# Where the prompt's softmax transposes stand in a neighbourhood-attention loop

## The chip, the cores and the metric

The kernel runs on one core of one Trainium2 chip. The metric is the device time of one execution in microseconds; the number given for a kernel is the median of its runs. Engines are called by the short names of the profile: PE (TensorE, matrix products and transposes), PEld (its weight loads), ACT (ScalarE), DVE (VectorE), POOL (GpSimd), SP (SyncE, here a queue of transfers).

## The reference, cut to what matters

Two layers work on 128 prompt tokens and 1024 sample tokens of width 1024. Layer 0 projects the tokens, runs a depthwise convolution branch (A) and an attention branch (B), gates both and projects back. Layer 1 is a pooling mixer. The change lies in branch B of layer 0, which has two parts with 8 heads of 64:

```python
# prompt: plain attention over the 128 prompt tokens
s = einsum('bqhd,bkhd->bhqk', q, k) * ATT_SCALE
o = einsum('bhqk,bkhd->bqhd', softmax(s), v)
# sample: a clamped 8 x 16 window on a grid of width 64, plus all context keys, in one softmax
s = concatenate([s_win + bias (masked), s_ctx]); p = softmax(s)
o = einsum(p_win, v_win) + einsum(p_ctx, v_ctx)
```

The sample's attention is far larger than the prompt's: 64 score tiles of 128 x 512 against 8 of 128 x 128.

## The kernel before, in words

The work before the attention (input projections, convolution, normalisation) and behind it (output projection of layer 0, layer 1) is nearly all matrix products on PE. The attention itself is a loop written out by hand, `attention_steps` (L1002). Heads are taken in 4 pairs (`pr`), each pair in 4 steps, so there are 16 steps `s` = 0 to 15 and a closing pass 16; `i` = `s % 4`.

A step `s` works on three things at once, in this order on PE:

- the scores of step `s + 1` (L879, 12 products of 128 x 512 into four "mm" banks; DVE adds the bias and takes the row minimum at L884; ACT takes the exponentials at L891; DVE and POOL normalise at L895 and L897);
- the values of step `s - 1` (L912, 32 products into one "cv" bank, which DVE multiplies into the gate at L923, the function `gate`);
- the transposes of the probabilities of step `s` (`turn`, L903): two tiles into the "tp" banks, which ACT copies out (L1055), one tile into a "cv" bank (ACT, L1061), and one more into a "tp" bank (DVE, L1062).

There are two "cv" and two "tp" banks, each handed out in turn, so a tile waits until the reader of the tile two before it in that tag is done.

Into each step two small pieces are woven. For pairs 0 to 2 these are five pieces that prepare the next pair (`prep`: transposes of its queries and keys) and three pieces of the prompt's attention (`prompt_attention`): `first` makes the two score tiles of the prompt (L937, one "cv" and one "tp" bank), DVE takes maxima (L939, L940), ACT the exponentials (L942), and then DVE and POOL normalise them (L945, L947) in a tile `pp`; `second` transposes `pp` on PE (L954) into one bank, and DVE copies it back (L955); `third` multiplies by the values (L960) and DVE gates the result (L965). A step has two places for a piece: place a, between the scores of the next step and the values ("cv" bank), and place b, ahead of the last transpose group ("tp" bank). In pairs 0 to 2 `first` stands in place b of the third step, `second` in place a of the fourth, `third` in place b of the fourth. In the last pair, which has no next pair to prepare, the three stand in place a of its first, second and third step (s = 12, 13, 14).

The order on PE, ACT and DVE inside the attention is the order in which the code issues (`manual_schedule`, L998). The order on POOL and on SP's transfer queue is made by a planner that goes by modelled times. From s = 10 on, the loop also converts the right half of the output weights (`load_right`, L1080 and on): POOL writes the high part (L1101), DVE the low part (L1102), from two buffers that SP refills (L1090) once both have read them. From s = 14 on, DVE and ACT also split the first output tiles (L1117, L1118), and in s = 15 and 16 PE does products of the output projection ahead (L1132).

Of the kernel before, what the change touches and what calls it, by code (L numbers as in the profile page):

```python
# [46 lines left out]
def _body(tc, nc, A, O, const, wp, arena, tmpp, smp, psp):  # L47
# [10 lines left out]
    def bank(tag):  # L58
        return psp.tile([P, 512], F32, tag=tag, bufs={"mm": 4, "tp": 2, "cv": 2}[tag], name=nm(tag))
# [123 lines left out]
    def split(raw, n=WUNIT, c=256):  # L183
        hi = wp.tile([P, WUNIT], F32R, tag="whi", bufs=4, name=nm("whi"))
        lo = wp.tile([P, WUNIT], F32R, tag="wlo", bufs=4, name=nm("wlo"))
        se.copy(hi[:, :n], raw[:, :n])  # L186
        ve.tensor_tensor(lo[:, :n], raw[:, :n], f(hi[:, :n]), ALU.subtract)  # L187
        return hi.rearrange("p (k c) -> p k c", c=c), lo.rearrange("p (k c) -> p k c", c=c)
# [563 lines left out]
    def bias_load(pr, hf):  # L752
        runs = ((0, 5), (5, 6), (6, 7), (7, 8)) if hf == 0 else ((0, 1), (1, 2), (2, 3), (3, 4), (4, 8))
        for e in range(2):
            h = 2 * pr + e
            for a, b in runs:
                off = 128 + RS[0][a] * 32 if hf == 0 else (RS[1][a] - 4) * 32
                m = 7 - DR0[hf][a]
                sy.dma_start(
                    bias[hf, e][a * 16 : b * 16, :, off : off + 256],  # L760
                    EX[m : m + b - a, :, :, h, :].rearrange("m q j k -> (m q) j k"),
                )
# [101 lines left out]
    def scores(step):  # L864


        pr, hf, j0 = step
        qh, ql, kh, kl, _ = qkT[pr]
        o = 0 if hf == 0 else 512
        ps, sts = [], []  # L870

        def matmuls(i):
            j = j0 + i
            bs = [bank("mm"), bank("mm")]
            qo = slice(hf * 512 + j * P, hf * 512 + (j + 1) * P)
            for n, (q, k) in enumerate(((qh, kh), (qh, kl), (ql, kh))):
                for e in range(2):
                    kv = k[H[e], o : o + 1024].rearrange("p (r c) -> p r c", c=64)[:, :, CB[j] : CB[j] + 32]
                    te.matmul(bs[e].rearrange("p (r c) -> p r c", c=32), q[H[e], qo], kv, start=(n == 0), stop=(n == 2))  # L879
            ps.append(wp.tile([P, 2, 512], F32, tag="whi", bufs=4, name=nm("p")))  # L880
            sts.append(small(8, "st"))
            for e in range(2):

                ve.tensor_tensor_reduce(  # L884
                    out=ps[i][:, e, :], in0=bs[e], in1=bias[hf, e][:, JT[j], :], scale=-1.0, scalar=3e38, op0=ALU.add, op1=ALU.min,
                    accum_out=sts[i][:, e : e + 1],
                )

        def exp(i, e):
            p, st = ps[i][:, e, :], sts[i]  # L890
            se.activation(p, p, AF.Exp, bias=st[:, e : e + 1], scale=-1.0, accum_out=st[:, 2 + e : 3 + e])  # L891

        def norm(i):
            st = sts[i]
            ve.reciprocal(st[:, 4:6], st[:, 2:4])  # L895
            for e in range(2):
                gp.tensor_scalar(ps[i][:, e, :], ps[i][:, e, :], st[:, 4 + e : 5 + e], 0.0, ALU.mult, ALU.add)  # L897

        return matmuls, exp, norm, ps

    def turn(tb, p):
        for x in range(4):
            te.transpose(out=tb[:, x * P : (x + 1) * P], in_=p[:, x * P : (x + 1) * P], identity=ident)  # L903
# [89 lines left out]
    def new_pt():  # L993
        return [wp.tile([P, 2, 512], F32, tag="wlo", bufs=4, name=nm("pt")) for _ in range(2)]
# [6 lines left out]
    def attention_steps():  # L1001

        nonlocal gr
        n = len(STEPS)
        sc_, vw, pts = {0: hold["S"]}, {0: hold["V"]}, {}
        right = load_right(0, (13, 15, 17, 2, 3, 4))
        for s in range(n + 1):
            i, pr = s % 4, s // 4  # L1010
            last_ = pr == 3
            nxt = None
            if s + 1 < n:
                nxt = sc_[s + 1] = scores(STEPS[s + 1])
                nxt[0](0)
                nxt[0](1)
                if pr < 3 and i in (0, 2):
                    bias_load(pr + 1, i // 2)
            if i == 0 and pr < 4:
                pieces = prep(pr + 1) if pr < 3 else []  # L1020
                prompt = prompt_attention(pr)
                ab = ([*prompt, None], [None] * 4) if last_ else ((pieces[0], pieces[2], pieces[4], prompt[1]), (pieces[1], pieces[3], prompt[0], prompt[2]))
            if s == n - 2:
                zs_part(0, 0)
            if s == n - 1:
                zs_part(0, 1)
                zs_part(1, 0)
                zs_part(1, 1)
            if s == n:
                out0_ahead(1)  # L1030
                units[L0_AT] = [split(*r) for r in raws[L0_AT]]
            if nxt:
                nxt[1](0, 0)
            a = ab[0][i]("cv") if s < n and ab[0][i] else None
            gate = values(STEPS[s - 1], pts.pop(s - 1), vw[STEPS[s - 1][0]]) if s else None
            if nxt:
                nxt[1](0, 1)
                nxt[1](1, 0)
            if a:
                a()  # L1040
            if nxt:
                nxt[2](0)
            if gate:
                gate()
            if s == n - 1:
                out0_ahead(0)
            if s == n:
                break
            ps = sc_.pop(s)[3]
            pt = pts[s] = new_pt()  # L1050
            tbs = [bank("tp"), bank("tp"), bank("cv")]
            for x in range(3):
                turn(tbs[x], ps[x // 2][:, x % 2, :])
            for x in range(2):
                se.copy(pt[0][:, x, :], tbs[x])  # L1055
            if nxt:
                nxt[1](1, 1)
            b = ab[1][i]("tp") if ab[1][i] else None
            tb = bank("tp")
            turn(tb, ps[1][:, 1, :])  # L1060
            se.copy(pt[1][:, 0, :], tbs[2])  # L1061
            ve.tensor_copy(pt[1][:, 1, :], tb)  # L1062
            if nxt:
                nxt[2](1)
            if b:
                b()
            if i == 2 and pr < 3:
                vw[pr + 1] = v_load(pr + 1)
            if n - 6 <= s < n - 1:
                hold["R"] = next(right)  # L1070
            if s == n - 3:
                gr = gr_tile()
                hold["gate"] = load_gates(0)
                y_of(0)
                y_of(1)
            if s == n - 2:
                raws[L0_AT] = load_raw(items[L0_AT][0])


    def load_right(l, ids, ahead=2):  # L1080


        hi = [slot(i, F32R, "wrh").rearrange("p (k c) -> p k c", c=512) for i in ids[:3]]
        lo = [slot(i, F32R, "wrl").rearrange("p (k c) -> p k c", c=512) for i in ids[3:]]
        rvs = []

        def load(k0):
            raw = wp.tile([P, WUNIT], F32, tag="raw", bufs=2, name=nm("raw"))
            rvs.append(raw.rearrange("p (k c) -> p k c", c=512))
            sy.dma_start(rvs[-1], A[f"w_out_{l}"][k0 * P : (k0 + 2) * P, 512:1024].rearrange("(k p) c -> p k c", p=P))  # L1090

        for k0 in range(0, 2 * ahead, 2):
            load(k0)
        yield hi, lo
        for k0 in range(0, 8, 2):
            rv = rvs[k0 // 2]
            for k in (k0, k0 + 1):
                if k % 2 and l:
                    se.copy(hi[k // 3][:, k % 3, :], rv[:, k - k0, :])
                else:  # L1100
                    gp.tensor_scalar(hi[k // 3][:, k % 3, :], rv[:, k - k0, :], 1.0, 0.0, ALU.mult, ALU.add)  # L1101
                ve.tensor_tensor(lo[k // 3][:, k % 3, :], rv[:, k - k0, :], f(hi[k // 3][:, k % 3, :]), ALU.subtract)  # L1102
            if k0 + 2 * ahead < 8:
                load(k0 + 2 * ahead)
            yield hi, lo
# [44 lines left out]
    def zs_part(t, kh):  # L1150
        g, a = t // 3, (t % 3) * P
        if t not in zs0:
            zs0[t] = [slot(i, F32R, "zs")[:, :D].rearrange("p (k t) -> p k t", t=P) for i in ((5, 8), (7, 9))[t % 2]]
        zpart(zs0[t], (zc, za)[kh][g][:, :, a : a + P], kh)

    def out0_ahead(t):

        first_out[t] = out_right(zs0[t], hold["R"])
# [200 lines left out]
    for i in range(len(items)):  # L1359
        a, b = ahead.get(i, (1, 2))  # L1360
# [35 lines left out]
```

## Time and profile before

| what | us |
|---|---|
| median of 3 runs (988.17 to 989.96) | 989.32 |
| profiled execution | 989.12 |
| its span, first to last instruction | 987.4 |
| PE busy | 949.5 (96%) |
| DVE busy | 603.0 (61%) |
| ACT busy | 404.9 (41%) |
| POOL busy | 368.4 (37%) |

PE is busy nearly throughout, so the time hangs on two things: how many microseconds PE works and where it stands still. The attention loop lies between about 443 and 563 us of the span. In the views, a line of the timeline gives the start, the length, the engine, the line of the code, the operation with its operands, the count of instructions merged into the row, and in brackets how long the engine was idle before it and what ended the wait. Matrix products are pipelined, so a merged row's length overlaps the next row's start a little; differences of starts are the safer measure.

### The profile page before, as it was taken

How to read it: one execution, taken by the hardware profiler on the slowest of the kernel's cores; microseconds unless marked ns; L12 is line 12 of the kernel's file. 1: busy time of each engine (PE TensorE's matmuls, PEld its weight loads, DVE VectorE, ACT ScalarE, POOL GpSimd, SP SyncE). 2: the span in 40 equal slices, each digit the busy share in tenths (PEclk: the TensorE clock that was granted, in tenths of full speed). 3: DMA queues.
4: the chain of work that ended last, by engine and by line, in shares of the span. 5: the costliest groups of instructions: out<-in, count | busy, mean ns of one | idle time of the engine just before them, and what ended most of it. 6: DMA issues, size and time to landing. Idle time of an engine off the chain costs nothing.

```text
span 987.4 us, 16652 instructions
## 1 busy us (share of the span) xinstructions
PE 949.5 (96%) x6388; PEld 863.0 (87%) x6388; DVE 603.0 (61%) x1243; ACT 404.9 (41%) x815; POOL 368.4 (37%) x485
## 2 busy tenths in 40 slices
PE   4887999999999999998998999999999999999998
PEld 2686988899999999986776788889999999998887
DVE  3577999999763444456776557566434545585332
ACT  3374666765411244238775423335222222231010
POOL 2264888998843301024455255341000000003322
PEclk8998999999999999999999999999999999999999
DMA  9969654226111111134334422151101111133311
GB/s 299 332 209 291 232 178 144 85 87 235 46 46 46 47 43 43 35 89 134 108 106 142 144 91 107 56 190 43 33 22 43 54 44 54 64 107 106 129 64 65
DMA packets 87531, 108.54 MB, mean 110 GB/s; under 512 B 10700, under 2 KB 73036, under 8 KB 87339
## 3 DMA queue, kind: packets, MB, share of 16 engines
q1 hardware_dynamic: 82539, 95.93, 30.6%
q0 software_dynamic: 2576, 9.18, 2.4%
q10 hardware_dynamic: 2336, 2.36, 0.7%
q8 instruction: 50, 0.82, 0.3%
q14 instruction: 30, 0.25, 0.1%
HBM read 94.64 MB, written 21.57 MB: 118 GB/s over the span
## 4 chain that ended last, share of the span: by engine, by line
PE 88%; DMA 7%; SPq 2%; DVE 1%; ACT 1%; issue 1%; POOL 1%; DVEq 0%; ACTq 0%; POOLq 0%
PE mm L232 37%; PE mm L239 16%; PE mm L1132 10%; PE mm L1125 10%; PE cv L912 3%; PE tp L903 2%; DMA wada<-in_w_ada 2%; PE mm L879 2%; PE mm L1295 2%; DMA tbias<-in_rpb 2%; PE tp L342 2%; DMA vwin<-in_cache_v 1%; DMA wad<-in_w_ada 1%; DMA raw<-in_w_out 1%; DMA raw<-in_w_in 1%; PE cv L903 1%
## 5 line engine op out<-in xcount | busy, mean ns | idle before, releaser
L232 PE MATMUL mm<-h,whi 128*128 128x384 f32 x1536 | 397.2, 338 | 1.7 <-ACT whi L186 1.4
L232 PEld LDWEIGHTS mm<-h,whi 128*128 128x128 f32 x1536 | 276.3, 188 | 9.0 <-ACT gr L474 2.6
L232 PE MATMUL mm<-h,wlo 128*128 128x384 f32 x768 | 257.3, 336 | 0.3 <-DVE wlo L187 0.3
L476 POOL TENSOR_TENSOR zc<-zc,gr 128x384 f32<-128x384 f32 x138 | 150.5, 1092 | 31.1 <-ACT gr L474 17.9
L239 PE MATMUL mm<-whi,h 128*128 128x256 f32 x864 | 157.1, 284 | 0.0
L232 PEld LDWEIGHTS mm<-h,wlo 128*128 128x128 f32 x768 | 144.3, 188 | 1.3 <-issue 0.7
L239 PEld LDWEIGHTS mm<-whi,h 128*128 128x128 f32 x864 | 135.1, 192 | 3.9 <-ACT gr L474 2.6
L239 PE MATMUL mm<-wlo,h 128*128 128x256 f32 x432 | 122.2, 283 | 0.0
L187 DVE TENSOR_TENSOR wlo<-raw,whi 128x1024 fp32r<-128x1024 f32 (+1 forms) x56 | 69.2, 1237 | 54.8 <-ACT whi L186 53.7
L487 DVE SCALAR_TENSOR_TENSOR cv<-u,convw,cv 128x384 f32<-128x384 f32 (+2 forms) x208 | 95.1, 513 | 0.9
L1132 PE MATMUL mm<-wrh,zs 128*128 128x512 f32 x288 | 92.4, 392 | 0.3 <-POOL wrh L1101 0.3
L1125 PE MATMUL mm<-whi,zs 128*128 128x512 f32 (+1 forms) x304 | 92.5, 379 | 0.0
L186 ACT CAST whi<-raw 128x1024 fp32r<-128x1024 f32 (+1 forms) x56 | 56.8, 1017 | 66.9 <-PE mm L232 23.6
L239 PEld LDWEIGHTS mm<-wlo,h 128*128 128x128 f32 x432 | 82.9, 192 | 0.0
L1139 POOL TENSOR_TENSOR y<-y,og 128x512 f32<-128x512 f32 x34 | 48.6, 1430 | 83.6 <-DVE og L1137 80.5
L474 ACT ACTIVATE gr<-u,convw 128x384 f32<-128x384 f32 (+2 forms) x128 | 64.3, 531 | 30.8 <-POOL zc L476 30.3
L897 POOL TENSOR_SCALAR p<-p,st 128x512 f32<-128x512 f32 x64 | 48.5, 771 | 49.6 <-DVE st L895 33.7
L1125 PEld LDWEIGHTS mm<-whi,zs 128*128 128x128 f32 x304 | 56.0, 188 | 10.7 <-issue 0.2
L1132 PEld LDWEIGHTS mm<-wrh,zs 128*128 128x128 f32 x288 | 53.9, 188 | 12.0 <-POOL wrh L1101 0.8
L1137 DVE TENSOR_TENSOR og<-mm,gr 128x512 f32<-128x512 f32 x34 | 23.3, 688 | 58.9 <-PE mm L1132 34.8
L1125 PE MATMUL mm<-wlo,zs 128*128 128x512 f32 (+1 forms) x152 | 57.2, 378 | 0.0
L456 ACT ACTIVATE th<-mm 128x384 f32<-128x384 f32 x48 | 23.5, 489 | 81.6 <-PE mm L232 81.5
(214 smaller groups left out, 1376.3 us busy)
## 6 DMA issues: line engine op xcount, KB each, us to landing
raw<-in_w_in SPq DMA_DIRECT2D x28, 512.0 KB
wad<-in_w_ada SPq DMA_DIRECT2D x16, 768.0 KB
wada<-in_w_ada SPq DMA_DIRECT2D x16, 512.0 KB
raw<-in_w_in SPq DMA_DIRECT2D x32, 256.0 KB
raw<-in_w_out SPq DMA_DIRECT2D x16, 512.0 KB
y0scr<-y POOLq DMA_DIRECT2D x9, 512.0 KB, 3.1
y<-y0scr SPq DMA_DIRECT2D x9, 512.0 KB
x<-in_x_sample SPq DMA_DIRECT2D x8, 512.0 KB
```

The lines of the kernel that those rows point to most:

```text
L186: se.copy(hi[:, :n], raw[:, :n])
L187: ve.tensor_tensor(lo[:, :n], raw[:, :n], f(hi[:, :n]), ALU.subtract)
L232: te.matmul(out, wsl(units, a, k, c0, P), hsl(hs, b, k, g), start=(k == 0 and i == 0), stop=(k == nk - 1 and i == 2))
L239: te.matmul(out, hsl(hs, p, k, g, a, P), wsl(units, q, k, 0, 256), start=(k == 0 and i == 0), stop=(k == 7 and i == 2))
L474: se.activation(pr[:, o : o + n], src, AF.Copy, scale=w)
L476: gp.tensor_tensor(z, z, pr, ALU.add)
L487: ve.scalar_tensor_tensor(zp if k == 30 else acc, src, convw[:, c, k : k + 1], zp if k == NPTS[c] else acc, ALU.mult, ALU.add)
L897: gp.tensor_scalar(ps[i][:, e, :], ps[i][:, e, :], st[:, 4 + e : 5 + e], 0.0, ALU.mult, ALU.add)
L903: te.transpose(out=tb[:, x * P : (x + 1) * P], in_=p[:, x * P : (x + 1) * P], identity=ident)
L1125: te.matmul(b[:, c0 : c0 + n], zs[p][:, k, :], WL[k // 2][q][:, k % 2, c0 : c0 + n], start=(k == 0 and i == 0), stop=(k == 7 and i == 2))
L1132: te.matmul(b, zs[p][:, k, :], WR[q][k // 3][:, k % 3, :], start=(k == 0 and i == 0), stop=(k == 7 and i == 2))
L1139: gp.tensor_tensor(yv, yv, t, ALU.add)
```

## The change

For pairs 0 to 2, `second` leaves place a of the fourth step and stands behind the values and the gate of that step, ahead of its transposes (a new, third place). Its copy on DVE is issued right behind it, and so stands behind the gate on DVE. `first` and `third` stay. In the last pair the three pieces take the same places as in the other pairs, without the idle steps between: `first` in place b of s = 12, `second` in the new place of s = 13, `third` in place b of s = 13. Nothing is computed more or less.

```diff
             if i == 0 and pr < 4:
                 pieces = prep(pr + 1) if pr < 3 else []
                 prompt = prompt_attention(pr)
-                ab = ([*prompt, None], [None] * 4) if last_ else ((pieces[0], pieces[2], pieces[4], prompt[1]), (pieces[1], pieces[3], prompt[0], prompt[2]))
+
+                if pr < 3:
+                    work = (pieces[0], pieces[2], pieces[4], None), (None, None, None, prompt[1]), (pieces[1], pieces[3], prompt[0], prompt[2])
+                else:
+                    work = (None,) * 4, (None, prompt[1], None, None), (prompt[0], prompt[2], None, None)
...
-            a = ab[0][i]("cv") if s < n and ab[0][i] else None
+            a = work[0][i]("cv") if s < n and work[0][i] else None
             gate = values(STEPS[s - 1], pts.pop(s - 1), vw[STEPS[s - 1][0]]) if s else None
...
             if gate:
                 gate()
+            if s < n and work[1][i]:
+                work[1][i]("cv")()
...
-            b = ab[1][i]("tp") if ab[1][i] else None
+            b = work[2][i]("tp") if work[2][i] else None
```

## Rows read from the trace of the kernel before

**Rows 1.** The page: the span.

```profile
span 987.4 us, 16652 instructions
```

**Rows 2.** Waits of PE from 443 to 562 us: us in total, times, longest.

```profile
PE cv L954 <- POOL pp L947: 3.4, 3, 1.1
```

**Rows 3.** Stages, steps 2, 3, 12, 13, 14: length, busy time by engine, PE clock, DMA.

```profile
454.32:460.85 6.53, 6.53 (x69) 5.08 (x68) 5.65 (x19) 5.35 (x14) 3.55 (x6) 1.00 0.78 218
460.85:468.62 7.77, 6.62 (x67) 4.95 (x66) 4.43 (x17) 5.22 (x17) 3.44 (x6) 1.00 0.45 125
...
523.75:532.69 8.94, 6.24 (x66) 4.93 (x65) 5.87 (x20) 4.97 (x15) 5.40 (x8) 0.97 0.79 261
532.69:539.86 7.17, 7.17 (x64) 5.45 (x63) 5.29 (x16) 4.27 (x12) 3.87 (x6) 0.80 0.24 82
539.86:546.63 6.77, 5.82 (x66) 4.71 (x65) 5.98 (x17) 5.23 (x14) 4.44 (x6) 1.00 0.42 111
```

**Rows 4.** Timeline of PE in step 3: start, length, what, idle before.

```profile
460.85 1.69 PE L879 MATMUL mm<-k,q 64*128 64x512 f32 x12
463.66 0.68 PE L954 MATMUL cv<-ident,pp 128*128 128x128 f32 x2 [1.12 <-POOL pp L947]
464.27 1.97 PE L912 MATMUL cv<-pt,gr 128*64 128x128 f32 x32
```

**Rows 5.** Timeline of ACT, POOL and DVE in step 3.

```profile
461.79 0.58 ACT L1061 COPY pt<-cv 128x512 f32<-128x512 f32 x1
...
463.23 0.73 POOL L947 TENSOR_SCALAR pp<-pp,st 128x128 f32<-128x128 f32 x2
...
466.28 0.49 DVE L923 TENSOR_TENSOR za<-cv,za 128x128 f32<-128x128 f32 x2 [1.10 <-PE cv L912]
```

**Rows 6.** Timeline of PE in steps 12 and 13.

```profile
530.03 0.63 PE L903 MATMUL tp<-ident,p 128*128 128x128 f32 x4 [1.89 <-ACT pp L942]
...
531.91 0.85 PE L903 MATMUL tp<-ident,p 128*128 128x128 f32 x4 [0.81 <-ACT pt L1055]
532.69 2.93 PE L879 MATMUL mm<-k,q 64*128 64x512 f32 x12
535.55 0.44 PE L954 MATMUL cv<-ident,pp 128*128 128x128 f32 x2
```

**Rows 7.** Timeline of DVE and ACT in step 12.

```profile
524.72 1.28 DVE L1102 TENSOR_TENSOR wrl<-raw,wrh 128x512 fp32r<-128x512 f32 x2
...
525.92 0.68 DVE L884 CUSTOM_DVE_ANT_0 p<-mm,bias 128x512 f32<-128x512 f32 x1
...
529.08 0.37 ACT L942 ACTIVATE pp<-cv,st 128x128 f32<-128x128 f32 x1 [1.62 <-DVE st L940]
```

**Rows 8.** Stages of one us in step 13: the clock is the third number from the end.

```profile
533.00:534.00 1.00, 1.00 (x6) 0.80 (x6) 1.00 (x3) 0.44 (x1) 0.35 (x1) 0.50 0.03 12
```

**Rows 9.** Timeline of DVE, ACT and PE in step 14.

```profile
542.16 0.68 DVE L884 CUSTOM_DVE_ANT_0 p<-mm,bias 128x512 f32<-128x512 f32 x1
...
545.02 1.04 ACT L1055 COPY pt<-tp 128x512 f32<-128x512 f32 x2
...
545.63 0.63 PE L903 MATMUL cv<-ident,p 128*128 128x128 f32 x4 [0.95 <-DVE st L895]
```

**Rows 10.** Timeline of POOL in steps 12 to 14.

```profile
524.71 2.44 POOL L897 TENSOR_SCALAR p<-p,st 128x512 f32<-128x512 f32 x2 [2.86 <-DVE st L895]
529.73 1.21 POOL L1101 TENSOR_SCALAR wrh<-raw 128x512 fp32r<-128x512 f32 x2 [2.58 <-DMA raw<-in_w_out]
...
531.62 1.37 POOL L897 TENSOR_SCALAR p<-p,st 128x512 f32<-128x512 f32 x2
...
538.54 1.21 POOL L1101 TENSOR_SCALAR wrh<-raw 128x512 fp32r<-128x512 f32 x2 [2.64 <-DMA raw<-in_w_out]
539.73 3.67 POOL L897 TENSOR_SCALAR p<-p,st 128x512 f32<-128x512 f32 x4
```

**Rows 11.** Waits of PE from 570 to 987 us.

```profile
PE tp L419 <- ACT h L424: 0.7, 1, 0.7
```

More of the change, by code (lines that the diff above doesn't have):

```diff
@@ L1010, in attention_steps @@
             i, pr = s % 4, s // 4
-            last_ = pr == 3
             nxt = None
```

## The prediction, made before the changed kernel was run

> **What bounds the kernel now.** I read the page first. PE is busy for 96% of the span, so only two things can move the time: PE's standing still, and PE at half clock. The waits of PE say where it stands. Inside the attention, PE waits three times for POOL's normalised prompt probabilities, 3.4 us in total [rows 2]. The stages by step show the same: step 3 takes 7.77 us where its neighbour, step 2, takes 6.53 with as much PE work [rows 3]; steps 7 and 11 repeat step 3 to within 0.01 us, so that row stands for three. Then come the first steps of the last pair: 8.94, 7.17 and 6.77 us, although they have less to do on PE than the others, because no next pair is prepared [rows 3]. The timeline shows why: in step 12, PE stands 1.89 us until ACT has taken the prompt's exponentials, and soon after 0.81 us more [rows 6]; then the granted clock falls to 0.50 of full, which is 1.2 instead of 2.4 GHz [rows 8], and the twelve score products take 2.93 us [rows 6] where they take 1.69 in step 3 [rows 4]. Behind the attention PE is held by almost nothing: its longest wait from 570 us to the end is 0.7 us [rows 11]. What PE gains in the loop is therefore kept to the end.
>
> **Part one, the fourth step of pairs 0 to 2 (steps 3, 7, 11).** `second` wants `pp`, which POOL writes from 463.23 to 463.96 [rows 5]; the scores ahead of it leave PE at 460.85 + 1.69 = 462.54 [rows 4]. PE stands 1.12 us, and as the halves of `pp` come one after the other, the two transposes then take 0.61 us from start to start (463.66 to 464.27) [rows 4]. Where `pp` lay ready, in step 13, the group lasted 0.44, of which about 0.37 before the next could start [rows 6]. Behind the values, which take 1.90 us (1.97 less the pipelined end [rows 4]), PE asks for `pp` at about 464.4, 0.4 us after it is there. So the wait goes: 1.12 + 0.61 - 0.37 = 1.36 us a step.
>
> What is late next? The values take over the "cv" bank that `second` had, and it comes free when ACT's copy ends at 461.79 + 0.58 = 462.37 [rows 5], just ahead of 462.54. The third transpose group then waits for the gate instead of for the copy of `pp`. The gate waited 1.10 us for PE at 466.28 [rows 5], so DVE is free for it at 465.2, and without the copy ahead of it 0.4 us earlier; it ends near 465.3, and the group is due at about 465.7. The copy follows the gate, ends near 465.7 and is asked for by `third` at 466.2. POOL has nothing added. I take 3 x 1.36 = 4.1 us. If the values had to wait for their bank, or `pp` came behind them, the gain would be halved, 2.0; at most it is 3 x (7.77 - 6.3) = 4.4, 6.3 being step 2 less a quarter of a microsecond that its transposes of the cached keys cost more than `second` (an estimate).
>
> **Part two, steps 12 to 14.** `first` moves from ahead of the values to place b. Before, its exponentials stood on ACT ahead of the step's second and third exponential and waited 1.62 us for DVE [rows 7], and with them the "tp" bank that the second transpose group wanted: that is the 1.89 us. In place b the group of `first` finds both banks free as in step 2. PE no longer stands there, so I also expect full clock: 2.93 - 1.69 = 1.24 us less in the scores alone. But not all of that is kept, for DVE is late in these steps: the weight conversion L1102 stands between DVE's last copy of a step and the next bias add. The chain is then scores, bias adds, exponentials, ACT's two copies, last transpose group, DVE's copy, L1102. Its terms: bias adds start 525.92 - 523.75 = 2.17 us behind the scores in step 12 [rows 3, 7] and 542.16 - 539.86 = 2.30 in step 14 [rows 3, 9]; from the first bias add to ACT's copies 545.02 - 542.16 = 2.86; the copies 1.04 [rows 9]; the last transpose group about 0.6 (a group of four took 0.63 at full clock [rows 6]). Step 12: 2.17 + 2.86 + 1.04 + 0.6 = 6.65. Step 13: the same, with the copy of `pp` and the gate of `third` partly on DVE's chain, 6.8. Step 14 loses `third` and the "cv" tile that made PE wait 0.95 us for DVE [rows 9], but its chain stays; before it took 6.77 [rows 3], I take 6.7. Sum 20.15 against 8.94 + 7.17 + 6.77 = 22.88: 2.7 us less.
>
> The bounds: DVE's busy time in the three steps is 5.87 + 5.29 + 5.98 = 17.1 us [rows 3], so at most 5.7 come back; at the other end the chain may hold the old 22.9, and nothing comes back. I take the value of the chain, as step 14 [rows 9] already runs at it.
>
> **One rule against it.** POOL's two normalisations took 2.44 us where DVE's L1102 ran beside them from 524.72, and 1.37 without it [rows 7, 10]. In the new step 13 the normalisation of `pp` falls next to the second pair of L1102, so up to 2.44 - 1.37 = 1.07 us could be added ahead of `second`; behind it stands the whole transpose group. I cost it at nothing, since the third group has to wait for the gate at about that time anyway; if that cover is gone, the saving is 5.7 instead of 6.8. The Trainium skill, page "SBUF — State Buffer", section "Who interferes with whom", says that a DVE instruction with two SBUF inputs and a GpSimd instruction that reads SBUF share a read interface, and that the one which comes second blocks fully; the trace agrees here, with 1.07 us added against a DVE row of 1.28.
>
> **The sum.** 4.1 + 2.7 = 6.8 us. The profiled execution took 989.12 us, of which the span is 987.4 [rows 1]; it lies 0.2 under the median of 989.32. 989.1 - 6.8 = 982.3.
>
> **The rivals.**
> - Only part one pays: the last pair is held by DVE and ACT as it was. For it: DVE is busy 5.3 to 6.0 us in each of these steps [rows 3]. Against: PE stood 2.7 us in step 12 for the banks of `first` alone [rows 6]. 989.1 - 4.1 = 985.0.
> - The last pair falls to what DVE has to do: 989.1 - 4.1 - 5.7 = 979.3. Against: the chain runs through ACT's copies and PE, which DVE waits for.
> - The shared read interface decides in step 13: 989.1 - 5.7 = 983.4.
> - The waits of part one are only halved (bank or `pp` late): 989.1 - 2.0 - 2.7 = 984.4.
> - The change does not do what it says: each wait comes back in another place of its step, for instance at the third transpose group, which now waits for the gate. 989.1.
> - Slower: POOL's queue in step 13. Its order is the planner's, and there the conversions L1101 have waited for their transfer 2.58 and 2.64 us with older work behind them, once ahead of four normalisations that took 3.67 [rows 10]. If that queue (1.21 + 3.67) stands ahead of `pp`: L1102 to the next L1101 took 529.73 - 524.72 = 5.01 us [rows 7, 10], so in the time of before, with L1102 at 531.4, L1101 starts at 536.4, the four follow and `pp` is there at 542.0, while PE wants it at 533.9: 8.1 us of standing still, and the clock falls again (1.24). 989.1 - 6.8 + 9.3 = 991.6. It decides from a `pp` that is 5.6 us late. Against: before, the planner put `pp` directly behind the first of these conversions and ahead of the second.
>
> **How the numbers follow.** Forecast 0.56, with its own range 981.2 to 983.5; only part one 0.15; the port 0.08; halved waits 0.06; the last pair at DVE's pace 0.06; no effect 0.04; slower 0.05. Leaving out a little on both sides, the range is 980.4 to 985.8: it holds the forecast, the port, the halved waits and most of "only part one". A measurement of this kernel can tell about 0.2%, or 2 us, from no change. Faster by more than that: all the cases under 987.3, with a little off for what I have not seen, 0.89; within it 0.06; slower 0.05.
>
> **What would show it.** In steps 3, 7 and 11: no wait of PE for POOL at `second`, the step at about 6.4 us, `second` between the values and the first transpose group. In step 12: no wait for ACT at the second transpose group, `first` ahead of the last group; from there to the end of step 14 a granted clock of 1.00; about 20.2 us from the scores of step 12 to the values of step 15. Wrong would be: a wait at the third group of these steps for the gate longer than 0.3 us, a wait of `second` for POOL in step 13, another half-clock stretch, or a new wait of PE behind the attention.

## The result and the profile after

The changed kernel took 982.93 us (median of 4 runs, 981.96 to 984.16) against 989.64 for the kernel before; the ratio is 0.9934, 95% interval [0.9918, 0.9949]. The prediction was 982.3. Two more comparisons gave 0.9937 [0.9923, 0.9951] and 0.9932 [0.9914, 0.9951]. (Comparisons use undisturbed runs alone.)

The stages of the changed kernel by step, columns as in [rows 3]: steps 2, 3, 12, 13 and 14.

```profile
455.99:462.51 6.52, 6.52 (x69) 5.08 (x68) 5.65 (x19) 5.33 (x14) 3.53 (x6) 1.00 0.78 218
462.51:468.70 6.19, 6.19 (x67) 4.90 (x66) 4.32 (x16) 5.22 (x17) 3.42 (x6) 1.00 0.45 121
520.66:527.44 6.78, 6.43 (x65) 5.08 (x65) 5.81 (x19) 4.42 (x13) 3.80 (x4) 1.00 0.74 224
527.44:534.55 7.11, 6.58 (x68) 4.91 (x68) 5.67 (x17) 5.13 (x17) 6.08 (x9) 1.00 0.50 188
534.55:540.90 6.35, 5.60 (x61) 4.49 (x60) 5.66 (x17) 4.36 (x11) 3.91 (x6) 1.00 0.38 115
```

Against [rows 3], step 2 is as it was, step 3 went from 7.77 to 6.19 us (steps 7 and 11 to 6.20 and 6.19), and steps 12 to 14 from 22.88 to 20.24, all at full clock. From the scores of step 1 to the values of step 15 the loop took 98.92 us before and 91.53 after, 7.39 less; in two further traces of the changed kernel it took 91.81 and 91.80. The profiled span fell by only 5.0 us: the loop began 1.66 us later in that trace, and the work behind it took 0.7 us longer. The instructions ahead of the loop are the same in both kernels and in the same order. The 0.7 us behind it is one wait, at the first product that wants the right half of the output weights of layer 1, before and after:

```profile
PE mm L1132 <- POOL wrh L1101: 0.3, 1, 0.3
```

```profile
PE mm L1137 <- POOL wrh L1106: 1.0, 1, 1.0
```

In the two further traces it was 0.16 and 0.45 us, and the work behind the loop took 440.63 and 440.97 us, against 440.77 before and 441.50 in the first trace.

The waits of PE inside the loop, changed kernel, columns as in [rows 2].

```profile
PE tp L816 <- ACT pt L1060: 1.3, 1, 1.3
PE tp L903 <- ACT pt L1060: 0.7, 1, 0.7
PE cv L954 <- POOL pp L947: 0.5, 1, 0.5
PE cv L937 <- DVE za L923: 0.3, 1, 0.3
```

The three waits of [rows 2] and the 1.89 us of [rows 6] are gone; the first row, in step 0, is as before. The second is in step 14 and the third in step 13; the last is `first` in step 12, which waits for the gate to free its "cv" bank. Step 3 on PE, then on POOL and DVE, answers to [rows 4, 5].

```profile
462.51 1.69 PE L879 MATMUL mm<-k,q 64*128 64x512 f32 x12
464.12 1.97 PE L912 MATMUL cv<-pt,gr 128*64 128x128 f32 x32
466.02 0.44 PE L954 MATMUL cv<-ident,pp 128*128 128x128 f32 x2
466.30 1.04 PE L903 MATMUL tp<-ident,p 128*128 128x128 f32 x8
```

```profile
464.88 0.72 POOL L947 TENSOR_SCALAR pp<-pp,st 128x128 f32<-128x128 f32 x2
...
466.43 0.46 DVE L923 TENSOR_TENSOR za<-cv,za 128x128 f32<-128x128 f32 x2
...
466.82 0.41 DVE L955 COPY pp<-cv 128x256 f32<-128x256 f32 x1
```

POOL writes `pp` until 465.60 and PE asks at 466.02: 0.42 us of cover, as forecast. Nothing on PE waits in this step.

Step 13 is the one that came out longer than forecast. Its rows on all engines:

```profile
527.63 1.21 POOL L1106 TENSOR_SCALAR wrh<-raw 128x512 fp32r<-128x512 f32 x2 [0.67 <-DMA raw<-in_w_out]
...
528.29 1.69 DVE L1107 TENSOR_TENSOR wrl<-raw,wrh 128x512 fp32r<-128x512 f32 x2
528.82 2.31 POOL L897 TENSOR_SCALAR p<-p,st 128x512 f32<-128x512 f32 x2
...
529.90 0.68 DVE L884 CUSTOM_DVE_ANT_0 p<-mm,bias 128x512 f32<-128x512 f32 x1
...
531.11 0.72 POOL L947 TENSOR_SCALAR pp<-pp,st 128x128 f32<-128x128 f32 x2
...
531.53 0.68 PE L954 MATMUL cv<-ident,pp 128*128 128x128 f32 x2 [0.51 <-POOL pp L947]
...
533.03 0.63 PE L903 MATMUL cv<-ident,p 128*128 128x128 f32 x4
```

PE does wait 0.51 us for `pp`, but the third transpose group (533.03) then stands behind the gate in any case. What is long is DVE's conversion (L1102 before, L1107 now): 1.69 us beside POOL's conversion and normalisations, where it took 1.28 in [rows 7]. So the bias adds begin 529.90 - 527.44 = 2.46 us behind the scores. The second trace shows that the wait for `pp` is not what makes the step long:

```profile
527.90 2.31 POOL L897 TENSOR_SCALAR p<-p,st 128x512 f32<-128x512 f32 x2 [0.27 <-DVE st L895]
...
528.02 1.71 DVE L1107 TENSOR_TENSOR wrl<-raw,wrh 128x512 fp32r<-128x512 f32 x2
...
529.66 0.68 DVE L884 CUSTOM_DVE_ANT_0 p<-mm,bias 128x512 f32<-128x512 f32 x1
...
530.62 0.68 PE L954 MATMUL cv<-ident,pp 128*128 128x128 f32 x2
...
532.79 0.63 PE L903 MATMUL cv<-ident,p 128*128 128x128 f32 x4 [0.62 <-DVE za L923]
```

There PE does not wait for `pp` at all, it waits 0.62 us for the gate instead, and the step took 7.38 us; the third trace is the same (0.62 and 7.36). DVE's conversion took 1.71 us beside POOL's normalisations alone, which had begun 0.12 us ahead of it; in [rows 7, 10] both began together, and it took 1.28.

### The profile page after: what moved, and what is told of

It is laid out like the page before. It is cut to its first block, busy times and chain, and to the rows that moved or that the text cites. A ratio compares the mean times of both kernels' runs of the same rounds, so it can differ in the third digit from the quotient of the medians.

```text
span 982.4 us, 16659 instructions
## 1 busy us (share of the span) xinstructions
PE 950.2 (97%) x6388; PEld 864.7 (88%) x6388; DVE 602.3 (61%) x1243; ACT 404.5 (41%) x815; POOL 367.9 (37%) x485
## 3 DMA queue, kind: packets, MB, share of 16 engines
q10 hardware_dynamic: 2336, 2.36, 0.7%
## 4 chain that ended last, share of the span: by engine, by line
PE 87%; DMA 8%; SPq 2%; ACT 1%; DVE 1%; issue 1%; POOL 0%; DVEq 0%; ACTq 0%; POOLq 0%
PE mm L232 37%; PE mm L239 16%; PE mm L1137 10%; PE mm L1130 10%; PE cv L912 3%; PE tp L903 2%; PE mm L879 2%; PE mm L1300 2%; DMA tbias<-in_rpb 2%; PE tp L342 2%; DMA raw<-in_w_out 1%; DMA wada<-in_w_ada 1%; DMA x<-in_x_sample 1%; DMA vwin<-in_cache_v 1%; DMA wad<-in_w_ada 1%; DMA raw<-in_w_in 1%
## 5 line engine op out<-in xcount | busy, mean ns | idle before, releaser
L186 ACT CAST whi<-raw 128x1024 fp32r<-128x1024 f32 (+1 forms) x56 | 56.9, 1017 | 66.6 <-PE mm L232 23.6
```

## The experiments

Ten kernels and two repeats of the changed kernel, each timed against the kernel before. A trace shows one execution, which can lie some us from the median.

**e1, part one alone.** The last pair as before: `work = (*prompt, None), (None,) * 4, (None,) * 4`.

> Part one alone: the prompt's second piece stands behind the values in pairs 0 to 2, the last pair as before. If the changed steps 3, 7 and 11 pay by themselves (7.77 to 6.19 us each in the trace after), the time is 989.6 - 4.7 = 984.9, PE's three waits of 1.1 us for POOL's prompt probabilities are gone, and steps 12 to 14 keep 8.9, 7.2 and 6.8 us with a half-clock stretch in step 13. If the gain of the change sits in the last pair, it stays within 1 us of 989.6.

Measured 986.11 against 990.01, ratio 0.9951 [0.9939, 0.9963], or 4.9 us less. Steps 3, 7 and 11 took 6.19, 6.20 and 6.20. The last pair, in rows of steps 12 and 13:

```profile
522.48:531.66 9.18, 6.47 (x65) 5.14 (x64) 5.88 (x20) 5.20 (x17) 5.62 (x8) 0.90 0.81 259
531.66:539.78 8.12, 8.12 (x64) 6.24 (x63) 5.29 (x16) 4.03 (x11) 4.47 (x7) 0.69 0.21 66
```

Part one pays by itself. The stall of step 12 is the same (1.90 and 0.81 us), but here it cost more than before: steps 12 to 14 took 23.75 us against 22.88, with the clock low for longer. The traced execution, at 991.78 us, was the slowest of the seven.

**e2, part two alone.** Pairs 0 to 2 as before: `work = (pieces[0], pieces[2], pieces[4], prompt[1]), (None,) * 4, (pieces[1], pieces[3], prompt[0], prompt[2])`.

> Part two alone: only the last pair has the new places. If it pays by itself, 989.6 - 2.6 = 987.0, steps 12 to 14 together 20.2 us instead of 22.9 with the full clock, steps 3, 7 and 11 still 7.77. If the two parts need each other, the time stays within 0.5 us of 989.6.

Measured 988.77 against 990.01, ratio 0.9983 [0.9973, 0.9993]: 0.7 to 2.7 us less. Steps 12 to 14 took 6.77 + 7.37 + 6.36 = 20.50 us at full clock, 2.4 less; steps 3, 7 and 11 kept their waits. The parts add: 4.7 (steps 3, 7 and 11 of e1) and 2.4 (steps 12 to 14 of e2) in the traces, 7.1 to 7.4 together; 4.9 and 1.7 in the times, 6.7 together.

**e3, only the first piece moved in the last pair.** `work = (None, prompt[1], prompt[2], None), (None,) * 4, (prompt[0], None, None, None)` there.

> The changed kernel, but in the last pair only the first piece has its new place; the second stands again ahead of the values of step 13 and the third ahead of those of step 14. If the places of the last pair work together, the second piece now makes PE stand some 2.4 us in step 13 (POOL writes the probabilities 2 to 2.7 us after the scores leave PE), step 12 stays at 6.8, step 13 grows to about 9 and the time is 982.9 + 1.9 = 984.8. If moving the first piece carries part two alone, it is 982.9 to 983.3.

Measured 985.79 against 990.01, 0.9951 [0.9939, 0.9963], the ratio of e1. PE in step 13:

```profile
530.41 0.80 PE L954 MATMUL cv<-ident,pp 128*128 128x128 f32 x2 [2.13 <-POOL pp L947]
531.13 3.46 PE L912 MATMUL cv<-pt,vw 128*64 128x128 f32 x32
```

Step 12 fell to 6.79, but PE now stands 2.13 us ahead of `second`, the values behind it run at half clock (3.46 us instead of 1.97; the granted clock was 0.50 from 531 to 534), and step 13 took 9.91. Moving `first` alone only moves the stall.

**e4, the first piece stays.** `work = (prompt[0], None, None, None), (None, prompt[1], None, None), (None, prompt[2], None, None)` in the last pair.

> The changed kernel, but in the last pair the first piece stands in its old place ahead of the values of step 12; second and third have the new places in step 13. If the exponentials of the first piece ahead of the step's own are the cause of the stall in step 12, the step is back at 8.9 us, the clock falls again in step 13, and the time is 982.9 + 1.7 to 982.9 + 2.2 = 984.6 to 985.1. If the stall came from the second and third piece, it stays at 982.9.

Measured 987.04 against 990.01, 0.9970 [0.9954, 0.9987]. The gain of 3.0 us is less than the 4.5 to 5.0 expected. Step 12 took 9.19 with waits of 1.90 and 0.81 us, the clock fell, and steps 12 to 14 took 24.03; the traced execution, at 991.84 us, was the slowest of the twelve. The place of `first` is the cause of the stall in step 12, and the new places of the other two don't help without it.

**e5, the kernel before with `pp` normalised on DVE.** `ve.tensor_scalar(...)` in place of `gp.tensor_scalar(...)` at L947, nothing moved.

> The kernel before in its old order, but the prompt's probabilities are normalised on DVE, right behind their reciprocal, and not on POOL behind two other normalisations. If their lateness is all that made PE stand in steps 3, 7 and 11, the second piece now starts about 1.1 us earlier without moving, each of these steps falls to about 6.5 us, and the time is 989.6 - 3.7 = 985.9. If the place of the piece matters by itself (its copy on DVE ahead of the gate, the bias adds 0.4 us later), less than 1 us is gained: 988.7 to 989.6.

Measured 987.09 against 988.67, 0.9984 [0.9974, 0.9994]. DVE and PE in step 3:

```profile
462.12 0.72 DVE L947 TENSOR_SCALAR pp<-pp,st 128x128 f32<-128x128 f32 x2
...
462.80 0.43 PE L954 MATMUL cv<-ident,pp 128*128 128x128 f32 x2 [0.27 <-DVE pp L947]
```

The steps took 6.74, 7.22 and 6.73, together 2.6 us less than before against the 3.7 expected: the lateness of `pp` is the larger share of the waits, but on DVE it still leaves 0.27 us of them (in step 7 twice). Behind the values there is none.

**e6, the weight conversion behind the gate.** In the changed kernel, `hold["R"] = next(right)` stands behind the new place for `second`, not at the end of the step.

> The changed kernel, with the conversion of the output weights in steps 11 to 14 moved from the end of the step to behind the gate, so that DVE does its part (1.3 to 1.7 us a step) while it waits for the last transposes and not ahead of the next bias adds. If that DVE work sets the length of steps 12 to 14, they fall from 6.78, 7.11 and 6.35 us to about 6.1, 6.4 and 5.7 and the time to 982.9 - 2.0 = 980.9. If exponentials, copies or POOL set it, the time stays at 982.9; if POOL's part comes late and now holds DVE's copies, it is 984 or more.

Measured 981.60 against 988.67, 0.9922 [0.9905, 0.9939]. Steps 12 and 14 fell to 6.05 and 5.55 as expected; step 13 rose to 7.99:

```profile
525.62 1.20 POOL L1106 TENSOR_SCALAR wrh<-raw 128x512 fp32r<-128x512 f32 x2 [4.51 <-DVE pt L1069]
...
526.81 2.70 POOL L897 TENSOR_SCALAR p<-p,st 128x512 f32<-128x512 f32 x4
...
529.48 0.72 POOL L947 TENSOR_SCALAR pp<-pp,st 128x128 f32<-128x128 f32 x2
...
529.91 0.68 PE L954 MATMUL cv<-ident,pp 128*128 128x128 f32 x2 [1.50 <-POOL pp L947]
```

POOL stood 4.51 us ahead of a conversion, with the four normalisations and `pp` queued behind it. That is the queue of the "slower" rival of the prediction, here at 1.50 us; but the row names a copy on DVE (L1069) as what ended POOL's wait, not the transfer that the rival had. Steps 12 to 14 took 19.59 us against 20.52 in the changed kernel on the same chip, and the times are not apart: 981.60 and 983.29, with intervals of the ratio that overlap.

**e7, e6 with the last pair's `pp` on DVE.** `(ve if pr == 3 else gp).tensor_scalar(...)` at L947.

> The changed kernel with the weight conversion behind the gate, as in the run before, and with the last pair's prompt probabilities normalised on DVE instead of on POOL. If POOL's queue made PE stand 1.50 us ahead of the second piece in step 13 there, that wait goes, step 13 falls from 7.99 to 6.3 to 6.6 us, the loop from the scores of step 1 to the values of step 15 from 90.9 to about 89.4, and the time to about 9 us under the kernel before. If DVE's two extra instructions only shift the wait to the bias adds, step 13 stays above 7.5.

Measured 982.80 against 989.11, 0.9941 [0.9925, 0.9956]. The wait for `pp` went, but step 13 took 7.02, not 6.3 to 6.6: the two normalisations took 0.93 us on DVE, ahead of the bias adds, which began 2.38 us behind the scores. Steps 12 to 14 took 18.62, 1.6 less than in the changed kernel, and the time did not show it: 6.3 us less than before, not 9. In this profile, of the slowest of the six executions (985.51), the clock fell once more behind the loop, after a wait of 1.24 us for the weights of layer 1.

**e8, the changed kernel with the last pair's `pp` on DVE.** The same edit in the changed kernel.

> The changed kernel, with the last pair's prompt probabilities normalised on DVE and nothing else changed. In the first trace of the change PE waited 0.51 us for POOL's probabilities in step 13. If that wait is covered by the gate and ACT's copies, as the prediction had it, step 13 stays at 7.1 to 7.4 us and the time within 0.5 us of the changed kernel. If it is on the path, step 13 falls to 6.6.

Measured 986.21 against 989.11, 0.9960 [0.9943, 0.9977]: some 2.5 us worse than the changed kernel by the ratios, whose intervals just overlap. Step 13:

```profile
529.06 0.71 DVE L947 TENSOR_SCALAR pp<-pp,st 128x128 f32<-128x128 f32 x2
...
529.69 1.70 DVE L1107 TENSOR_TENSOR wrl<-raw,wrh 128x512 fp32r<-128x512 f32 x2
...
531.31 0.68 DVE L884 CUSTOM_DVE_ANT_0 p<-mm,bias 128x512 f32<-128x512 f32 x1
...
534.44 0.63 PE L903 MATMUL cv<-ident,p 128*128 128x128 f32 x4 [1.78 <-DVE za L923]
```

The wait for `pp` is gone and the step is 8.57 us long. The bias adds begin 3.47 us behind the scores, PE stands 1.78 us for the gate, and the clock falls (0.50 from 536 to 538). Neither branch of the expectation came about: both left out what 0.71 us more on DVE costs ahead of the bias adds.

**e9, the stall filled with work.** In the kernel before, `for i in (0, 1, 0, 1) if step == STEPS[11] else (0, 1):` makes the value products of step 12 twice.

> The kernel before, but in step 12 the 32 value products are done twice into the same bank (the second pass overwrites the first), so that PE works 1.9 us of the 1.9 us in which it stood for the prompt's exponentials. If the standing still is what lowers the granted clock in step 13, the clock stays at 1.00 there, the twelve score products take 1.7 instead of 2.9 us, and steps 12 to 14 take 22.0 to 22.6 instead of 22.9 us. If the clock falls all the same, the steps take 22.9 or more.

Measured 988.33 against 989.11, 0.9992 [0.9982, 1.0002]. Steps 12 to 14, and the doubled products:

```profile
523.94:532.67 8.73, 7.78 (x98) 6.62 (x97) 5.88 (x20) 4.76 (x15) 5.20 (x8) 1.00 0.75 261
532.67:538.77 6.10, 6.09 (x64) 4.66 (x63) 5.19 (x16) 4.37 (x12) 3.13 (x4) 1.00 0.30 106
538.77:545.22 6.45, 5.83 (x66) 4.71 (x65) 5.66 (x17) 5.23 (x14) 5.47 (x8) 1.00 0.45 126
```

```profile
525.79 3.71 PE L912 MATMUL cv<-pt,vw 128*64 128x128 f32 x64
```

With more work the three steps take 21.28 us instead of 22.88: the granted clock stays at 1.00, and the old step 13 takes 6.10 instead of 7.17. So the low clock of step 13 goes with the standing still: with products in its place it did not come (one trace of each kernel). Of the 1.6 us, 1.3 are in steps 12 and 13; the other 0.3 are in step 14, at full clock in both kernels, where DVE's conversion took 1.27 us here and 1.60 before. The low clock cost the kernel before 1.3 us directly and at most 1.6; the interval of the total time is too wide to confirm so small a sum.

**e10, both shares of the conversion out of the way.** e6, with POOL's share (L1101 before) on ACT, at the end of the step before: `se.copy(hi[...], rv[...])`, a `yield` between high and low part.

> The changed kernel with DVE's part of the weight conversion behind the gate, as in two runs before, and POOL's part of it moved to ACT, at the end of the step before. If POOL's queue (conversions that wait for their transfer, with the normalisations behind them) is what kept step 13 at 7.0 to 8.0 us there, no wait of PE for POOL is left in steps 12 to 14, they take about 6.1, 6.3 and 5.6 us, 18.0 together against 20.2 in the changed kernel, and the time is 2 us under it: about 8.5 under the kernel before. If ACT, with 1.2 us more a step, now sets the step, they take 6.7 or more each and nothing is gained.

Measured 982.75 against 989.62, 0.9933 [0.9920, 0.9946]. The stages:

```profile
520.96:527.00 6.04, 6.03 (x66) 4.79 (x65) 5.87 (x18) 5.59 (x14) 3.88 (x5) 1.00 0.91 301
527.00:533.37 6.37, 6.37 (x67) 4.88 (x66) 5.80 (x19) 6.04 (x19) 4.18 (x7) 1.00 0.44 170
533.37:538.94 5.57, 5.57 (x62) 4.53 (x61) 5.39 (x16) 5.53 (x14) 2.81 (x5) 1.00 0.56 168
```

PE no longer waits for anything in these steps, which take 17.98 us against the expected 18.0. Yet the median is only 1.0 us under that of the changed kernel on the same chip, and the ratios are the same. A shorter loop is shown; a faster kernel is not.

**The changed kernel, second and third time.**

> The changed kernel once more, for a second trace of it: steps 3, 7 and 11 at 6.2 us, steps 12 to 14 at 6.8, 7.1 and 6.4, time 982.9. If the 1.7 us by which its attention began later in the first trace belong to the change, they are there again; if they are the spread of the start, whose first 100 us hang on transfers, they differ.

> The changed kernel again, on the same chip as the run above and with the same runs of the kernel before, so that the two can be compared: steps 12 to 14 together 20.2 to 20.6 us, 6.4 us under the kernel before.

983.29 against 988.67 and 983.77 against 989.62. Steps 12 to 14 took 20.52 and 20.51 us. Step 1 began at 448.86 and 449.33, at 449.37 in the first trace and at 447.71 before. Over all traces the start differs by up to 3.7 us, and not evenly: in the four of kernels with the old order in pairs 0 to 2 (before, e2, e5, e9) it lies between 447.71 and 447.94, in the ten with the new order between 447.50 (e6) and 451.18 (e1), in nine of them at 448.51 or later. All of the difference arises in the first 100 us, where the instructions are the same. So the record leans to a later start that goes with part one and takes back some of what the loop gains; e6 shows that it need not come, and its cause stays open.

## Why the prediction was right, step by step

- **Part one** was forecast at 4.1 us (1.36 a step), measured at 1.58 a step, 4.7. The wait went where the forecast said, and `pp`, the bank, the gate and the copy were in time. Two sizes were off, which made the forecast too small: `second` holds PE for 0.28 us (466.02 to 466.30), not 0.37, and the wait by starts was 463.66 - 460.85 - 1.61 = 1.20, not the 1.12 of the row, with 1.61 the way from scores to values in step 3 of the changed kernel. The stated upper limit of 4.4 was passed too: it allowed 6.3 us for the step, a quarter of a microsecond under step 2, and the step takes 6.19 against 6.52.
- **Part two** was forecast at 2.7 us and measured at 2.64, 2.36 and 2.37 in three traces. The mechanism for step 12 held (6.65 forecast, 6.78 measured; the "cv" bank for `first` was not quite free, a wait of 0.26 us), and e3 and e4 show that it takes `first` and `second` together. Steps 13 and 14 were off in opposite ways. Step 13 took 7.11 to 7.38, not 6.8: the forecast let POOL's normalisations be slowed by DVE's conversion, but not the conversion by POOL (1.69 for 1.28). Step 14 took 6.35, not 6.7: its last transpose group waits only for the first of ACT's two copies, as no `third` takes a bank in between (539.64, group at 540.35).

```profile
535.52 1.28 DVE L1107 TENSOR_TENSOR wrl<-raw,wrh 128x512 fp32r<-128x512 f32 x2
536.72 0.68 DVE L884 CUSTOM_DVE_ANT_0 p<-mm,bias 128x512 f32<-128x512 f32 x1
...
539.64 1.05 ACT L1060 COPY pt<-tp 128x512 f32<-128x512 f32 x2
540.35 0.63 PE L903 MATMUL tp<-ident,p 128*128 128x128 f32 x4 [0.75 <-ACT pt L1060]
```

- **The chain through DVE** is shown by step 13 in four traces of three kernels. The bias adds begin 2.38 us (e7), 2.46 (changed), 2.73 (changed, second trace) and 3.47 (e8) behind the scores, and the step takes 7.02, 7.11, 7.38 and 8.57. In the first three the difference is 4.64 or 4.65; in e8 it is 5.10, with part of the step at half clock. In e10 they begin 1.52 us behind the scores and the step is 6.37, all of it PE's work.
- **The clock** was forecast as 1.24 us in the scores, not all kept. By e9 it is 1.3 to 1.6 of the 2.4 to 2.6 us of part two; the rest is about 1.
- **The port** (1.07 us, costed at nothing): POOL's pair of normalisations took 2.31 us and `pp` came 0.51 us late in the first trace, and step 13 did not hang on it: without that wait it took 7.38 and 7.36. The price came by the other end, through DVE's conversion.
- **The slower rival** did not come about: the planner again put `pp` right behind the normalisations of step 13. e6 shows that the same queue can hold it.
- **The signs of being wrong** that the prediction named came in part: `second` waited 0.51 us for POOL in step 13 (first trace), the third group waited 0.62 us there for the gate (second and third trace), and behind the attention a wait of 0.3 us grew to 1.0 (first trace). None cost more than 0.7 us. But "what PE gains in the loop is therefore kept to the end" does not hold as it stands.
- **The forecast of the total** is better than its terms, and that part is luck: the loop gained 7.1 to 7.4, not 6.8, the loop began 1.2 to 1.7 us later, and the work behind it took 0.1 less to 0.7 us more. The medians fell by 6.7, 5.4 and 5.9 us.

## What to carry to other kernels

A piece that waits for a slow engine belongs behind work that is ready, not ahead of it; the gain is the wait, plus what a low clock behind a long wait costs. Moving one piece of a chain only moves the wait, so the pieces have to move together. Before giving an idle-looking engine more work, look where its next instruction stands: in step 13, 0.71 us on DVE cost 1.2 us or more (e8), since the bias adds behind it start the chain of the step. And a gain inside a loop is to be followed to the end of the kernel: here a start and a wait outside the loop took part of it back.

## What was not expected of the hardware

The same stall in step 12 (1.9 and 0.8 us) cost differently in four traces: steps 12 to 14 took 22.88 us in the kernel before and in e5, 23.75 in e1 and 24.03 in e4; in e1 the clock stood at 0.50 through the six slices of one us from 530 to 536, in the kernel before only in two, and in part of two more. Waits of 1.1 us (steps 3, 7, 11), 1.34 (step 0) and 1.50 (e6) inside the loop were not followed by a lower clock, waits of 1.78 (e8), 1.89 and 2.13 (e3) were.

Behind the loop, PE waited 1.24 us for the weights of layer 1 in five traces (e1, e2, e4, e6, e7). The clock stayed at 1.00 in e2 and e6 and fell to 0.50 in e1, e4 and e7. Those three are also the ones in which PE had waited 0.30 to 0.37 us for a weight conversion on ACT (L186), 1.7 us earlier; e2 and e6 have no such wait. Here e7:

```profile
882.01 0.50 PE L1130 MATMUL mm<-whi,zs 128*128 128x512 f32 x1 [0.32 <-ACT whi L186]
...
883.75 0.50 PE L1137 MATMUL mm<-wrh,zs 128*128 128x512 f32 x1 [1.24 <-POOL wrh L1106]
```

```profile
885.00:886.00 1.00, 1.00 (x3) 0.77 (x3) 0.00 (x0) 0.00 (x0) 0.00 (x0) 0.50 0.95 367
```

The work behind the loop took 443.8 to 444.8 us in these three traces and 440.6 to 442.3 in the other eleven, and each of the three is the slowest execution of its kernel, 2.7 to 5.7 us over the median. So this place can give back what the loop gains in one execution and not in the next, which fits e6 (442.3) and e7 (444.8), though not e10 (441.2), whose loops are shorter and whose times are not clearly so. That the waits there are the cause is not shown: removing them was not tried.
